# Turning and splitting the embedding's input p on VectorE during the second group of projections, and loading the parts from memory

## The chip, the cores and the metric

The kernel runs on one core of one Trainium2 chip. A core has a matrix engine (TensorE, PE in the profile; PEld is its loading of weights), VectorE (DVE), ScalarE (ACT), GpSimd (POOL) and SyncE (SP), which run beside one another and wait for each other by semaphores, and 16 DMA engines that move data between HBM and the core's memory. Matmuls write to PSUM; the other operands lie in SBUF. SP, ACT and POOL issue the DMAs, each on a queue of its own. The metric is the device time of one execution in microseconds; lower is better.

## The reference

One layer of a streaming encoder on 2048 prompt frames and 32 frames of running streams (2080 in all, 1024 wide), in fp32:

```python
hn = rmsnorm(h, g_mix)
proj = hn @ w_in                                  # (2080, 1024) @ (1024, 3072)
hA, bA, cA, zA, vB, zB = split(proj)              # a gated convolution and a pooling mixer
yA = bA * short_conv(cA * hA) * silu(zA)
yB = (pool_groups(vB) @ pool_w * pool_scale) * silu(zB)
h = h + concat(yA, yB) @ w_out                    # (2080, 1024) @ (1024, 1024)
gate = sigmoid(rmsnorm(h, g_ple) @ w_ple_gate)    # (2080, 1024) @ (1024, 1024)
h = h + (p @ w_ple) * gate                        # p: (2080, 256), w_ple: (256, 1024)
y = rmsnorm(h, g_final)
```

The change is about `p @ w_ple`, the embedding e, and about p, its input. The states of the two mixers are outputs too.

## The kernel before

Frames are handled in 17 tiles: 16 of 128 frames and one of 32. Every fp32 operand of a matmul is split in two parts of a narrower kind: `split` (L75 to L81) lets ACT copy the value to the first part (L77) and DVE subtract that from the value to give the second (L80). A product is then three matmuls, part by part. The large products go further: two by two blocks are multiplied in the manner of Strassen with seven products in place of eight (`seven`), from sums of blocks that DVE prepares.

The stages, in order of time. First, frames are normalised and turned (to 31 us). The projections follow in three groups of frame blocks, `GROUPS = [[0, 1], [2, 3], [4]]`, each with four units of output columns: group 0 to 233 us, group 1 to 427, and the plain group 2, which is block 4 alone, to 539. Then come three early tiles of the embedding (to 548), the output projection (PE line L169, to 710), the other embedding tiles but one (to 750; 12 full tiles and the short one), the gate of the short tile (`gl`, to 759) and the gate of the full tiles in pairs (to 921). The last pair (`last_pair`, L1459 ff) computes tile 15's embedding itself.

The matmuls want p with its 256 columns on the partitions. `embed` (L106 to L152) does this for a list of tiles: `prep` loads rows of p for four tiles in one DMA on SP (L123, L126), PE transposes a tile in two pieces of 128 by 128 into PSUM (L132, tile `ptp`), and `split` makes the parts `pps` from there. `run` keeps two tiles ahead, multiplies (`embed_product`, L101 to L104: two halves of 512 columns, six matmuls each), copies the result out of PSUM on ACT (L149) and writes it to e_d (L150), from where the gate stage loads it. It is called for the early tiles (`early_embedding`), for the rest (`rest_e`), and the last pair has its own copy (`embedded`, L1479).

What runs beside the units' matmuls in the projections is a generator that `at_pace` advances by a given share of steps at fixed places of a unit. In group 1, from unit j = 1 on, it is `last_block` (L1150 ff): it normalises and turns the four tiles of block 4 and writes them to b_d in memory, one step in three calls. Group 2 then loads b_d into `hn` by two DMAs on POOL's queue (L1183). The raw weights of each unit are loaded by SP and split by ACT and DVE some way ahead of PE; buffers are given out in rings (`ring4`), and a load waits until the ring's oldest buffer is free.

A scheduler orders the instructions of each engine, but an engine takes its own in order, and so do the queues: an instruction that waits holds up all behind it on its engine. Sums of squares go from ACT to POOL, which makes 1/rms from them (L69, L73); POOL also issues many of the DMAs.

For the gate, the rows of w_gate are loaded by POOL, scaled by ACT and written to g_d (`scale_gate`, L1287 to L1292), loaded again as raw weights `wg_r` by SP (L1385) and split and summed by DVE and ACT during the embedding. The frames' rows h come back from h_d: `turned` (L1388 to L1401) has PE turn them (`pth`, L1399), and `turned_here` (L1403 to L1412) loads them with 32 partitions to a piece (L1408) and has DVE turn blocks of 32 by 32 in place (`nc.vector.transpose`, L1410, STREAM_TRANSPOSE in the profile). Since blocks alone are turned, rows of the weights are taken in the order that fits, which is why w_gate is loaded by the pattern `(q k c) n -> k q c n`.

SBUF pools that the change touches: xin (5 buffers of 128x1024, rows of frames during the projections), ya (5), xh (3), cmb (8), st (4 buffers for `pps` and sums), ss (3).

Of the kernel before, what the change touches and what calls it, by code (L numbers as in the profile page):

```python
# [9 lines left out]
F32 = mybir.dt.float32  # L10
# [5 lines left out]
P = 128  # L16
D = 1024
# [17 lines left out]
def trunk(ctx, tc, x_p, x_s, c_conv, c_pool, p_p, p_s, g_mix, w_in, conv_w, conv_b, pool_w,  # L35
# [8 lines left out]
    h_d = tc.dram_tile([T, D], F32, name="h_d")  # L44
    e_d = tc.dram_tile([T, D], F32, name="e_d")
    g_d = tc.dram_tile([D, D], F32, name="g_d")

    const = ctx.enter_context(tc.tile_pool(name="const", bufs=1))
    ps_m = ctx.enter_context(tc.tile_pool(name="ps_m", bufs=6, space=PSUM))
# [5 lines left out]
    def tbank(name):  # L55
        return ps_t.tile([P, 512], F32, tag="tr", name=name)
# [46 lines left out]
            for q, (a, b) in enumerate(((0, 0), (0, 1), (1, 0))):  # L103
                nc.tensor.matmul(ps[:n], pps[:, a, k, :n], wp[k][b][:, cs], start=k + q == 0, stop=k == 1 and q == 2)  # L104

    def embed(todo, wp, ring, queue=nc.sync):  # L106

        got = {}

        def prep(c):
            if c in got or c >= len(todo):
                return
            i = todo[c]
            r, n = tiles[i]
            if c % 4 == 0:
                pt = ring("p", i)
                m = min(4, len(todo) - c)  # L120
                full = [j for j in todo[c:c + m] if j < NT - 1]
                if full:
                    nc.sync.dma_start(pt.rearrange("p (a d) -> p a d", a=4)[:, :len(full)],  # L123
                                      p_p[r:r + len(full) * P].rearrange("(a p) d -> p a d", p=P))
                if len(full) < m:
                    nc.sync.dma_start(pt[:DEC, len(full) * PLE:(len(full) + 1) * PLE], p_s)  # L126
                got["p"] = pt
            pt = got["p"][:, (c % 4) * PLE:(c % 4 + 1) * PLE]
            pps = ring("pps", i)
            ptp = tbank(f"ptp_{i}")  # L130
            for k in range(2):
                nc.tensor.transpose(ptp[:, k * P:k * P + n], pt[:n, k * P:(k + 1) * P], ident[:n, :n])  # L132
            v = ptp.rearrange("p (k t) -> p k t", k=4)[:, :2, :n]
            split(pps[:, 0, :, :n], pps[:, 1, :, :n], v)
            got[c] = pps

        def run(c, last=False):
            i = todo[c]
            r, n = tiles[i]
            prep(c)  # L140
            prep(c + 1)
            prep(c + 2)
            pps = got[c]
            o = ring("out", i)
            for nh in range(2):
                cs = slice(nh * NH, nh * NH + NH)
                ps = bank(f"e_{i}_{nh}")
                embed_product(ps, pps, wp, cs, n)
                (nc.vector.tensor_copy if last and nh else nc.scalar.copy)(o[:n, cs], ps[:n])  # L149
            (nc.gpsimd if last else queue).dma_start(e_d[r:r + n], o[:n])  # L150

        return prep, run  # L152
# [170 lines left out]
    def load_bottom(k, t):  # L323
        return nc.sync.dma_start(t, w_out[(KH + k) * P:(KH + k + 1) * P])

    def load_rows(pool, name, i, pr, sa=None):
        r, n = tiles[i]
        t = ring4(pool, f"{name}_{i}")
        nc.sync.dma_start(t[:n], pr[r:r + n] if sa is None else rows_of(pr, sa, r, n))
        return t  # L330

    with ExitStack() as s1:
# [768 lines left out]
        def embedding_weights(name):  # L1101
            wp = []
            for k in range(2):
                raw = ring4(raws, f"raw_{name}{k}")
                nc.sync.dma_start(raw, w_ple[k * P:(k + 1) * P])
                t = [wtile(f"{name}{k}_{h}").rearrange("p k h n -> p (k h n)") for h in range(2)]
                split(t[0], t[1], raw)
                wp.append(t)
            return wp
# [39 lines left out]
        def last_block():  # L1149

            load_ahead(2, 0)
            for c in range(4):
# [5 lines left out]
                for half in range(2):  # L1158
                    pt = turn(x, half, f"pt4_{c}_{half}", later=True)
                    to_memory(b_d[:, half * KH:half * KH + KH], f"b_4_{c}_{half}", pt, c * P, x[1])  # L1160
                    yield

        def at_pace(steps, num, den):

            calls = [0]

            def step():
                calls[0] += num
                while calls[0] >= den:
                    calls[0] -= den  # L1170
                    next(steps, None)

            return step

        B = B0
        for gi, tbs in enumerate(GROUPS):
            if gi == 2:

                frames_in.close()
                t = slot("hn_4")  # L1180
                hn[4] = piece_of(t, 0), piece_of(t, 1)
                for half in range(2):
                    nc.gpsimd.dma_start(hn[4][half].bitcast(F32), b_d[:, half * KH:half * KH + KH])  # L1183
                W = sums_slots("wo")
                nc.sync.dma_start(g_bc, g_fin.partition_broadcast(P))
                ya = ctx.enter_context(tc.tile_pool(name="ya", bufs=5, side="right"))
                first_y = load_y(0, 2 * P)
                first_x = load_rows(ya, "x", 0, x_p)
                tops = [ring4(ya, f"wo_q{i}") for i in range(2)]
                for k in range(KH):  # L1190
                    load_top(k, tops[k // 2])
            if gi == 1:
                B = load_group(1)
            for j in range(4):
                unit = gi * 4 + j
                u = Unit(gi, tbs, j)
                if unit == 0:
                    u.plain()
                    B0["T4"] = piece_of(seventh("B0_T4"), 0)
                    nc.sync.dma_start(B0["T4"].bitcast(F32), p_d["T4"])  # L1200
                    p_d["T4"] = tc.dram_tile([P, KH, 2, NB], F32, name="p_dT4b")
                    aside = at_pace(next_columns(3, 0, 1, 2), 39, 56)
                elif gi == 0:
                    u.seven(B, aside)
                elif gi == 1:
                    if j == 1:
                        aside = at_pace(last_block(), 1, 3)
                    u.seven(B, aside, j == 0)
                else:
                    u.plain()  # L1210
                if gi == 2:
                    early_sums(j)
# [5 lines left out]
    with ExitStack() as s2:  # L1218
# [48 lines left out]
            S[i], more = frame_parts(cmb, ss, f"y{i}", lo[:, :, :P], hi[:, :, :P], lo[:, :, P:], hi[:, :, P:])  # L1267
            return more

        def short(name, parts, n):  # L1270
            A = []
            for half, t in enumerate(parts):
                c = cmb.tile([P, KH, 2, P], F32R, tag="c", name=f"{name}_{half}")
                c = c.rearrange("p k h n -> p k (h n)")
                split(c[:, :, :n], c[:, :, n:2 * n], t[:, :, :n])
                A.append(c)
            return A
# [74 lines left out]
        def embedding_chunks(name):  # L1352
            wp = []
            for k in range(2):
                raw = ring4(ya, f"{name}r_{k}")
                nc.sync.dma_start(raw, w_ple[k * P:(k + 1) * P])
                t = [cmb.tile([P, KH, 2, P], F32R, tag="c", name=f"{name}_{k}_{h}").rearrange("p a b c -> p (a b c)")
                     for h in range(2)]
                split(t[0], t[1], raw)
                wp.append(t)  # L1360
            return wp
# [9 lines left out]
                return cmb.tile([P, D], F32, tag="c", name=f"eout_{i}")  # L1371
            return ring4(ya, f"e{what}_{i}")

        _, run = embed(rest_e, wp, ring)
        for c in range(len(rest_e) - LATE):
            run(c)

# [1 line left out]
        W = sums_slots("wg")  # L1379
        quarters("wg", W)  # L1380
        for k in range(KH):
            raw = [ring4(xh, f"wg_r{k}_{i}") for i in range(2)]
            for i in range(2):
                kk = i * KH + k
                nc.sync.dma_start(raw[i], g_d[kk * P:(kk + 1) * P])  # L1385
            whole_quarters(W, k, *raw)
            weight_sums(W, k, *raw)

        def turned(i):

            r, n = tiles[i]
            t = load_rows(ya, "hn", i, h_d).rearrange("p (q k c) -> p k q c", q=4, k=KC)
            out = []
            for half in range(2):
                pt = tbank(f"pth_{i}_{half}")
# [7 lines left out]
        def turned_here(i):  # L1403
# [1 line left out]
            r, n = tiles[i]  # L1405
            t = ring4(ya, f"hn_{i}")
            for q in range(4):
                nc.sync.dma_start(t[q * 32:q * 32 + 32].rearrange("p (g c) -> p g c", g=4),  # L1408
                                  h_d[r:r + P, q * 256:q * 256 + 256].rearrange("(g p) c -> p g c", p=32))
            nc.vector.transpose(t, t)  # L1410
            u = t.rearrange("p (g k t) -> p k g t", g=4, k=KC)
# [47 lines left out]
        def last_pair(i, A):  # L1459
# [1 line left out]

            pt = ring4(ya, "p_l")[:, :PLE]
            nc.sync.dma_start(pt, p_p[(i + 1) * P:(i + 2) * P])
            e = load_rows(ya, "e", i, e_d)
            wp = embedding_chunks("wl")
            h = [load_rows(xh, "h", i + b, h_d) for b in range(2)]
# [2 lines left out]
            hg = [ring4(ya, f"hg_{b}") for b in range(2)]  # L1471
            sums = [[], []]
            gate = {}

            def embedded():
                pps = ss.tile([P, 2, 2, P], F32R, tag="s", name="pps_l")
                ptp = tbank("ptp_l")
                for k in range(2):
                    nc.tensor.transpose(ptp[:, k * P:k * P + P], pt[:, k * P:(k + 1) * P], ident)  # L1479
                split(pps[:, 0], pps[:, 1], ptp.rearrange("p (k t) -> p k t", k=4)[:, :2])  # L1480
                return pps

            def finish(b, half, ee, m):

# [40 lines left out]
                embed_product(ps, pps, wp, slice(half * NH, half * NH + NH))  # L1525
                finish(1, half, ps, m)

            pps = embedded()
            seven(f"g{i}", A, W, carry, out, {5: lambda: second(1, NH)}, first_tile=True)
            second(0, NH // 2)  # L1530

# [36 lines left out]

        S = {}
        n = tiles[NT - 1][1]  # L1570
        A = short("gl", turned(NT - 1), n)
        for step in prep_g(0).values():
            step()
        for c in range(len(rest_e) - LATE, len(rest_e)):
            run(c)
        h, e = (load_rows(*a) for a in ((xh, "h", NT - 1, h_d), (ya, "e", NT - 1, e_d)))
# [39 lines left out]
```

## Time and profile before

| What | us |
|---|---|
| Median of 3 runs | 931.7 (931.09 to 933.5) |
| Profiled execution, device time | 930.71 |
| Its span in the profile | 928.9 |
| PE busy | 916.0 (99%), 4581 instructions |
| DVE busy | 716.7 (77%) |
| ACT busy | 483.7 (52%) |
| POOL busy | 127.5 (14%) |
| DMA packets | 133791, 190.05 MB, mean 205 GB/s |
| PE clock granted | 0.998 of full speed |

The span runs from the first to the last instruction of the profile, and the device time has 1.8 us more around it. A line of the timeline or of a group gives start, duration, engine, line of the kernel, operation and output <- inputs by the program's names; in brackets stands the idle time before it with what ended that. PE's durations overlap, because matmuls are pipelined; the distance from start to start tells what one costs. A line of the waits gives who waited for whom: us in total, times, the longest. A line of the windows gives a stretch, its length, each engine's busy time with its instructions, the clock, the mean busy share of the 16 DMA engines and GB/s.

### The profile page before, as it was taken

How to read it: one execution, taken by the hardware profiler on the slowest of the kernel's cores; microseconds unless marked ns; L12 is line 12 of the kernel's file. 1: busy time of each engine (PE TensorE's matmuls, PEld its weight loads, DVE VectorE, ACT ScalarE, POOL GpSimd, SP SyncE). 2: the span in 40 equal slices, each digit the busy share in tenths (PEclk: the TensorE clock that was granted, in tenths of full speed). 3: DMA queues.
4: the chain of work that ended last, by engine and by line, in shares of the span. 5: the costliest groups of instructions: out<-in, count | busy, mean ns of one | idle time of the engine just before them, and what ended most of it. 6: DMA issues, size and time to landing. Idle time of an engine off the chain costs nothing.

```text
span 928.9 us, 13088 instructions
## 1 busy us (share of the span) xinstructions
PE 916.0 (99%) x4581; PEld 827.6 (89%) x4581; DVE 716.7 (77%) x1215; ACT 483.7 (52%) x895; POOL 127.5 (14%) x244
## 2 busy tenths in 40 slices
PE   8999999999999999999999999999999999999996
PEld 7999999999999999999999987888878868888885
DVE  7996989999487778585777679655564797888985
ACT  7734565654345544443544356344334865555664
POOL 3011232211001110000000011112111001111113
PEclk9999999999999999999999999999999999999999
DMA  9257687798935457247665369666775883666563
GB/s 271 81 153 220 175 258 224 220 297 321 388 98 177 127 177 222 87 116 257 194 178 169 127 219 300 216 214 199 224 210 184 313 261 120 217 224 229 192 209 114
DMA packets 133791, 190.05 MB, mean 205 GB/s; under 512 B 11740, under 2 KB 101084, under 8 KB 132445
## 3 DMA queue, kind: packets, MB, share of 16 engines
q1 hardware_dynamic: 117741, 138.78, 47.7%
q0 software_dynamic: 13248, 44.93, 14.9%
q10 hardware_dynamic: 2736, 5.51, 1.9%
q8 instruction: 36, 0.59, 0.3%
q14 instruction: 30, 0.25, 0.1%
HBM read 129.59 MB, written 59.58 MB: 204 GB/s over the span
## 4 chain that ended last, share of the span: by engine, by line
PE 80%; DVE 4%; DMA 2%; ACT 1%; issue 1%; POOL 1%; SPq 0%; POOLq 0%; DVEq 0%; ACTq 0%
PE x_o L169 9%; PE x_g L169 9%; PE x_zab L580 6%; PE x_ch L580 5%; PE x_zbv L580 5%; PE e L104 5%; PE z_g L169 5%; PE z_o L169 4%; PE z_ch L580 3%; PE z_zab L580 3%; PE z_zbv L580 2%; PE y_g L169 2%; PE y_o L169 2%; PE b L580 2%; PE v L580 2%; PE c L580 2%
## 5 line engine op out<-in xcount | busy, mean ns | idle before, releaser
L77 ACT CAST y_S<-y_fS 128x512 fp32r<-128x512 f32 x32 | 19.6, 623 | 43.3 <-PE x_o L169 19.4
L104 PE MATMUL e<-wq,pps 128*128 128x512 f32 (+1 forms) x156 | 38.9, 399 | 0.2 <-ACT pps L77 0.2
L169 PE MATMUL x_g<-wg_b,g_S 128*128 128x512 f32 x128 | 36.0, 390 | 0.0
L169 PE MATMUL x_o<-wo_b,y_S 128*128 128x512 f32 x128 | 35.8, 391 | 0.0
L580 PE MATMUL x_zbv<-B,w_zbv_S 128*128 128x416 f32 x168 | 34.3, 352 | 0.0
L580 PE MATMUL z_ch<-B,w_ch_S 128*128 128x416 f32 x168 | 34.2, 352 | 0.0
L580 PE MATMUL z_zbv<-B,w_zbv_S 128*128 128x416 f32 x168 | 34.1, 351 | 0.0
L580 PE MATMUL x_zab<-B,w_zab_S 128*128 128x416 f32 x168 | 34.1, 351 | 0.0
L580 PE MATMUL z_zab<-B,w_zab_S 128*128 128x416 f32 x168 | 34.1, 351 | 0.0
L580 PE MATMUL x_ch<-B,w_ch_S 128*128 128x416 f32 x168 | 34.0, 351 | 0.0
L104 PEld LDWEIGHTS e<-wq,pps 128*128 128x128 f32 (+1 forms) x156 | 27.4, 182 | 6.9 <-ACT pps L77 0.5
L580 PEld LDWEIGHTS x_ch<-B,w_ch_S 128*128 128x128 f32 x168 | 31.4, 188 | 0.3
L580 PEld LDWEIGHTS z_zbv<-B,w_zbv_S 128*128 128x128 f32 x168 | 31.3, 188 | 0.3
L580 PEld LDWEIGHTS x_zab<-B,w_zab_S 128*128 128x128 f32 x168 | 31.3, 188 | 0.3
L580 PEld LDWEIGHTS z_zab<-B,w_zab_S 128*128 128x128 f32 x168 | 31.3, 188 | 0.3
L580 PEld LDWEIGHTS z_ch<-B,w_ch_S 128*128 128x128 f32 x168 | 31.3, 188 | 0.4
L580 PEld LDWEIGHTS x_zbv<-B,w_zbv_S 128*128 128x128 f32 x168 | 31.2, 188 | 0.4
L69 POOL TENSOR_SCALAR ms_f<-ssq_f 128x1 f32<-128x1 f32 (+1 forms) x15 | 8.8, 587 | 161.3 <-ACT junk L90 161.3
L77 ACT CAST y<-y 128x512 fp32r<-128x512 f32 x24 | 14.9, 620 | 29.2 <-PE x_o L169 14.0
L414 DVE SCALAR_TENSOR_TENSOR xt<-xt,rstd_x,g_bc 128x1024 f32<-128x1024 f32 (+2 forms) x14 | 17.9, 1280 | 15.3 <-POOL rstd_x L73 14.1
L1438 DVE SCALAR_TENSOR_TENSOR h<-h,rstd_f,g_bc 128x1024 f32<-128x1024 f32 (+1 forms) x15 | 19.3, 1284 | 12.7 <-POOL rstd_f L73 12.7
L169 PEld LDWEIGHTS x_o<-wo_b,y_S 128*128 128x128 f32 x128 | 24.0, 188 | 5.1 <-ACT c_o L1242 0.3
(583 smaller groups left out, 2664.2 us busy)
## 6 DMA issues: line engine op xcount, KB each, us to landing
y<-y_d SPq DMA_DIRECT2D x16, 512.0 KB, 10.5
x<-in_x_prompt_dram SPq DMA_DIRECT2D x16, 512.0 KB, 6.3
h_d<-x SPq DMA_DIRECT2D x16, 512.0 KB, 4.2
h<-h_d SPq DMA_DIRECT2D x16, 512.0 KB, 3.6
xt<-in_x_prompt_dram SPq DMA_DIRECT2D x15, 512.0 KB, 7.3
e<-e_d SPq DMA_DIRECT2D x15, 512.0 KB, 5.8
out_dram<-h POOLq DMA_DIRECT2D x14, 512.0 KB, 3.0
p_dT<-T POOLq DMA_DIRECT2D x12, 512.0 KB, 6.1
```

Source lines behind the costliest of these rows:

```text
L69: nc.gpsimd.tensor_scalar(ms[:n], ssq[:n], scalar1=1.0 / D, scalar2=EPS, op0=ALU.mult, op1=ALU.add)
L77: ins = nc.scalar.copy(hi, src)
L104: nc.tensor.matmul(ps[:n], pps[:, a, k, :n], wp[k][b][:, cs], start=k + q == 0, stop=k == 1 and q == 2)
L169: nc.tensor.matmul(ps[:n], lhs[:, k, a, :n], w[b][:, k], start=start and k + q == 0, stop=k == KH - 1 and q == 2, skip_group_check=True)
L414: nc.vector.scalar_tensor_tensor(xt[:n], xt[:n], r[:n], g_bc[:n], op0=ALU.mult, op1=ALU.mult)
L580: nc.tensor.matmul(ps[:, :NB], lhs[:, k, x], b[:, k, y], start=start and k + q == 0, stop=stop and k == KH - 1 and q == 2, skip_group_chec ...
L1438: nc.vector.scalar_tensor_tensor(h[:n], h[:n], rf[:n], g_bc[:n], op0=ALU.mult, op1=ALU.mult)
```

## The change

p is turned and split once, during group 1, and the parts are kept in memory (pp_d). A generator `turn_p` follows `last_block` in group 1, and the two together advance one step in two calls. It works in five rounds, four of four tiles and one of the short tile. POOL's queue loads p's rows in four pieces of 32 partitions, DVE turns blocks of 32 by 32 in place (128x1024, or 128x64 for the short tile), ACT and DVE split tile by tile, and POOL's queue writes each tile's parts, 256 KB, to pp_d. The next round's load is issued behind the turn of the one before.

In the embedding, `prep` only loads a tile's parts from pp_d: on SP for the three early tiles, on POOL's queue for the others, on SP for the last pair's. `run` looks four tiles ahead in place of three. The transposes L132 and L1479, their PSUM tiles and the splits behind them are gone. The rows of w_ple are loaded in the order that the turned blocks have (`ple_rows`).

To make room and order for this, the raw weights of the gate take buffers of ya and xh in turn in place of xh alone, the short gate's parts lie in ya in place of cmb, and the first loads of hn for the gate (short tile and first pair) go to POOL's queue, later ones to SP as before. Since turn_p keeps xin in use until its end, the pool ya, which takes the same room, and with it the first loads of y, x and wo_q for the output projection, begin later in SP's order: behind raw_v of group 2, where they stood between the raw weights of unit 3 before.

```diff
+    pp_d = tc.dram_tile([NT, P, 2 * PLE], F32, name="pp_d")
...
+    ple_rows = w_ple.rearrange("(q k c) n -> k q c n", q=4, k=2)
+
+    def load_pps(t, i, queue):
+        n = tiles[i][1]
+        queue.dma_start(t.rearrange("p a k n -> p (a k) n")[:, :, :n].bitcast(F32),
+                        pp_d[i].rearrange("p (a n) -> p a n", a=4)[:, :, :n])
+        return t
...
-    def embed(todo, wp, ring, queue=nc.sync):
+    def embed(todo, wp, ring, queue=nc.sync, loads=nc.sync):
...
-            ptp = tbank(f"ptp_{i}")
-            for k in range(2):
-                nc.tensor.transpose(ptp[:, k * P:k * P + n], pt[:n, k * P:(k + 1) * P], ident[:n, :n])
-            v = ptp.rearrange("p (k t) -> p k t", k=4)[:, :2, :n]
-            split(pps[:, 0, :, :n], pps[:, 1, :, :n], v)
-            got[c] = pps
+            if c not in got and c < len(todo):
+                got[c] = load_pps(ring("pps", todo[c]), todo[c], loads)
...
-            prep(c)
-            prep(c + 1)
-            prep(c + 2)
+            for ahead in range(4):
+                prep(c + ahead)
...
-                nc.sync.dma_start(raw, w_ple[k * P:(k + 1) * P])
+                nc.sync.dma_start(raw, ple_rows[k])
...
+        def turn_p():
+
+            def load(a):
+                t = ring4(xin, f"p_{a}")
+                for q in range(4):
+                    part, cs = t[q * 32:q * 32 + 32], slice(q * 64, q * 64 + 64)
+                    if a < NT - 1:
+                        nc.gpsimd.dma_start(part.rearrange("p (m c) -> p m c", c=64),
+                                            p_p[a * P:(a + 4) * P, cs].rearrange("(m p) c -> p m c", p=32))
+                    else:
+                        nc.gpsimd.dma_start(part[:, :64], p_s[:, cs])
+                return t
+
+            rounds = [*range(0, NT - 1, 4), NT - 1]
+            t = load(0)
+            yield
+            for a, after in zip(rounds, rounds[1:] + [None]):
+                w = D if a < NT - 1 else 64
+                nc.vector.transpose(t[:, :w], t[:, :w])
+                v = t[:, :w]
+                if after is not None:
+                    t = load(after)
+                yield
+                for b in range(0, 4 if w == D else 1, 2):
...
+                        split(hi, lo, src)
+                        nc.gpsimd.dma_start(pp_d[i].rearrange("p (a n) -> p a n", a=4)[:, :, :n],
+                                            o.rearrange("p a k n -> p (a k) n").bitcast(F32))
                     yield
...
-                        aside = at_pace(last_block(), 1, 3)
+                        aside = at_pace(chain(last_block(), turn_p()), 1, 2)
...
-        _, run = embed(rest_e, wp, ring)
+        _, run = embed(rest_e, wp, ring, loads=nc.gpsimd)
...
-            raw = [ring4(xh, f"wg_r{k}_{i}") for i in range(2)]
+            raw = [ring4(t, f"wg_r{k}_{i}") for i, t in enumerate(((ya, ya), (ya, xh), (xh, xh), (ya, ya))[k])]
...
+        hn_queue = [nc.gpsimd]
...
-            pt = ring4(ya, "p_l")[:, :PLE]
-            nc.sync.dma_start(pt, p_p[(i + 1) * P:(i + 2) * P])
+            pps = load_pps(ss.tile([P, 2, 2, P], F32R, tag="s", name="pps_l"), i + 1, nc.sync)
...
-            pps = embedded()
             seven(f"g{i}", A, W, carry, out, {5: lambda: second(1, NH)}, first_tile=True)
...
-        A = short("gl", turned(NT - 1), n)
+        A = short("gl", turned(NT - 1), n, ya)
         for step in prep_g(0).values():
             step()
+        hn_queue[0] = nc.sync
```

More of the change, by code (lines that the diff above doesn't have):

```diff
@@ L104, in embed_product @@
                 nc.tensor.matmul(ps[:n], pps[:, a, k, :n], wp[k][b][:, cs], start=k + q == 0, stop=k == 1 and q == 2)
-    def embed(todo, wp, ring, queue=nc.sync):
+    ple_rows = w_ple.rearrange("(q k c) n -> k q c n", q=4, k=2)
[5 more added lines that the diff above has]
+    def embed(todo, wp, ring, queue=nc.sync, loads=nc.sync):
         got = {}
         def prep(c):
[L114 to L129, printed above, removed]
-            ptp = tbank(f"ptp_{i}")
-            for k in range(2):
-                nc.tensor.transpose(ptp[:, k * P:k * P + n], pt[:n, k * P:(k + 1) * P], ident[:n, :n])
-            v = ptp.rearrange("p (k t) -> p k t", k=4)[:, :2, :n]
-            split(pps[:, 0, :, :n], pps[:, 1, :, :n], v)
-            got[c] = pps
+            if c not in got and c < len(todo):
+                got[c] = load_pps(ring("pps", todo[c]), todo[c], loads)
         def run(c, last=False):
@@ L324, in load_bottom, with load_rows @@
         return nc.sync.dma_start(t, w_out[(KH + k) * P:(KH + k + 1) * P])
-    def load_rows(pool, name, i, pr, sa=None):
+    def load_rows(pool, name, i, pr, sa=None, queue=nc.sync):
         r, n = tiles[i]
         t = ring4(pool, f"{name}_{i}")
-        nc.sync.dma_start(t[:n], pr[r:r + n] if sa is None else rows_of(pr, sa, r, n))
+        queue.dma_start(t[:n], pr[r:r + n] if sa is None else rows_of(pr, sa, r, n))
         return t
@@ L1161, in last_block @@
                     yield
+        def turn_p():
[20 more added lines that the diff above has]
+                for b in range(0, 4 if w == D else 1, 2):
+                    s = staged(f"pps_{a + b}").rearrange("p a h n -> p (a h n)")
+                    for c in range(2 if w == D else 1):
+                        i = a + b + c
+                        n = tiles[i][1]
+                        o = s[:, c * 2 * PLE:(c + 1) * 2 * PLE].rearrange("p (a k n) -> p a k n", a=2, k=2)[:, :, :, :n]
+                        if n == P:
+                            src = v[:, (b + c) * PLE:(b + c + 1) * PLE].rearrange("p (g k r) -> p k g r", g=4, k=2)
+                            hi, lo = (o[:, h].rearrange("p k (g r) -> p k g r", g=4) for h in range(2))
+                        else:
+                            src = v.rearrange("p (k r) -> p k r", k=2)
+                            hi, lo = o[:, 0], o[:, 1]
+                        split(hi, lo, src)
+                        nc.gpsimd.dma_start(pp_d[i].rearrange("p (a n) -> p a n", a=4)[:, :, :n],
+                                            o.rearrange("p a k n -> p (a k) n").bitcast(F32))
+                    yield
         def at_pace(steps, num, den):
@@ L1268, in prep_h, with short @@
             return more
-        def short(name, parts, n):
+        def short(name, parts, n, pool=None):
             A = []
+            if pool is not None:
+                both = pool.tile([P, 2, KH, P], F32R, tag="t", name=f"{name}_a")
             for half, t in enumerate(parts):
-                c = cmb.tile([P, KH, 2, P], F32R, tag="c", name=f"{name}_{half}")
-                c = c.rearrange("p k h n -> p k (h n)")
+                c = (cmb.tile([P, KH, 2, P], F32R, tag="c", name=f"{name}_{half}").rearrange("p k h n -> p k (h n)")
+                     if pool is None else both[:, half])
                 split(c[:, :, :n], c[:, :, n:2 * n], t[:, :, :n])
@@ L1355, in embedding_chunks @@
                 raw = ring4(ya, f"{name}r_{k}")
-                nc.sync.dma_start(raw, w_ple[k * P:(k + 1) * P])
+                nc.sync.dma_start(raw, ple_rows[k])
                 t = [cmb.tile([P, KH, 2, P], F32R, tag="c", name=f"{name}_{k}_{h}").rearrange("p a b c -> p (a b c)")
@@ L1387, in trunk @@
             weight_sums(W, k, *raw)
+        hn_queue = [nc.gpsimd]
         def turned(i):
             r, n = tiles[i]
-            t = load_rows(ya, "hn", i, h_d).rearrange("p (q k c) -> p k q c", q=4, k=KC)
+            t = load_rows(ya, "hn", i, h_d, queue=hn_queue[0]).rearrange("p (q k c) -> p k q c", q=4, k=KC)
             out = []
@@ L1407, in turned_here @@
             for q in range(4):
-                nc.sync.dma_start(t[q * 32:q * 32 + 32].rearrange("p (g c) -> p g c", g=4),
+                hn_queue[0].dma_start(t[q * 32:q * 32 + 32].rearrange("p (g c) -> p g c", g=4),
                                   h_d[r:r + P, q * 256:q * 256 + 256].rearrange("(g p) c -> p g c", p=32))
@@ L1473, in last_pair @@
             gate = {}
[L1475 to L1481, printed above, removed]
             def finish(b, half, ee, m):
```

## The prediction

> **What bounds the kernel now.** I read the page first, then TensorE's waits, then the timeline of the stretch that the change shortens. The page has TensorE (PE) busy for 916.0 of 928.9 us:
>
> ```profile
> span 928.9 us, 13088 instructions
> ...
> PE 916.0 (99%) x4581; PEld 827.6 (89%) x4581; DVE 716.7 (77%) x1215; ACT 483.7 (52%) x895; POOL 127.5 (14%) x244
> ```
>
> The chain of waits gives PE 80%. PE's own waits, by what ended them, are short and nearly all early:
>
> ```profile
> PE gm L376 <- DVE V L813: 2.3, 1, 2.3
> PE zb L608 <- DVE B L654: 0.8, 1, 0.8
> PE y_o L164 <- ACT wo_c L1308: 0.5, 1, 0.5
> ...
> PE e L104 <- ACT pps L77: 0.2, 1, 0.2
> ```
>
> So the time is the sum of what PE issues. Work taken off PE counts in full, and work put on other engines costs nothing until PE waits for it. The timeline of PE from 704 us shows what the transposes of p cost there (start, length, line, what, count; lengths overlap, so I go by the distance of starts):
>
> ```profile
> 704.74 2.88 PE L169 MATMUL z_o<-wo_d,y_S 128*128 128x512 f32 x12
> 707.46 2.89 PE L169 MATMUL x_o<-wo_T,y 128*128 128x512 f32 x12
> ...
> 710.19 0.60 PE L132 MATMUL ptp<-ident,ep 128*128 128x128 f32 x4
> 711.03 0.96 PE L104 MATMUL e<-wq,pps 128*128 128x512 f32 x3 [0.24 <-ACT pps L77]
> ...
> 717.14 0.38 PE L132 MATMUL ptp<-ident,ep 128*128 128x128 f32 x2
> 717.27 3.00 PE L104 MATMUL e<-wq,pps 128*128 128x512 f32 x12
> 720.11 0.38 PE L132 MATMUL ptp<-ident,ep 128*128 128x128 f32 x2
> ```
>
> Twelve matmuls of 512 columns take 707.46 − 704.74 = 2.72 us in the output projection. A tile of the embedding has the same twelve and a pair of transposes, and takes 720.11 − 717.14 = 2.97 us. A pair costs **0.25 us**: 0.14 of its own and 0.11 by which the matmuls behind it start later.
>
> **What is removed from PE.** The order of the changed program's instructions has none of the 17 pairs: 13 in the embedding's main stretch, 3 in its early tiles, one in the last pair of gate tiles. 17 × 0.25 = 4.25 us. The main stretch also loses its first wait: the last of the four transposes at 710.19 starts at 710.51 and its follower at 711.03, 0.52 us against the 0.07 between others, so 0.45 more. Sum **4.7 us**. From above: the stretch is 40.24 us (710.19 to 750.43); less 156 matmuls at 0.2267 = 35.37, and less 0.61 for the eight transposes of hn at 744.19, it leaves 4.26 for 13 pairs and the wait, which with 4 × 0.25 for the others is 5.3. From below: if the matmuls behind a pair start late for a reason that stays, 17 × 0.14 + 0.45 = 2.8. I take 4.7, since 2.97 against 2.72 repeats at every tile. The 17 ACT copies (375 ns) and 17 DVE subtracts (422 ns) also leave these stretches; neither bounds them, ACT being busy 32.07 of 40 us there and DVE 29.02.
>
> **What is added, in the second group (277 to 427 us).** DVE: four stream transposes of 128x1024, by the same instruction on hn (1237 ns), one short, and 17 subtracts of 128x256. 4 × 1.24 + 0.2 + 17 × 0.42 = 12.3 us; ACT 17 × 0.375 = 6.4. Room, by windows (PE, PEld, DVE, ACT, POOL busy):
>
> ```profile
> 290.00:325.00 35.00, 35.00 (x192) 34.49 (x191) 26.77 (x41) 19.09 (x34) 5.21 (x8) 1.00 0.54 160
> 325.00:360.00 35.00, 35.00 (x191) 33.69 (x190) 26.54 (x44) 15.92 (x30) 4.86 (x6) 1.00 0.55 157
> 360.00:393.00 33.00, 33.00 (x176) 32.67 (x176) 22.50 (x40) 14.03 (x26) 0.00 (x0) 1.00 0.55 176
> 393.00:427.00 34.00, 34.00 (x182) 33.66 (x181) 25.80 (x38) 15.00 (x26) 1.12 (x2) 1.00 0.52 179
> ```
>
> DVE idles 35.4 us from 290 to 427, and PE never does. What is queued behind a round of the new work is the weights' splits. They end 9 to 13 us before PE's first matmul on them (w_zbv_S: split done 331.00, first used 339.99; most others 11.6 to 13.1), and that lead is nearly constant, so it is set by buffers that PE gives back, not by DVE. A round is 1.24 + 4 × 0.42 = 2.9 us, inside it. I take nothing; the end on the other side is all 12.3 us on PE. POOL's loads and writes of p (some 0.5 to 1 us to issue each, as b_d's writes) add p's 2.1 MB and 4.2 MB of writes to a stretch where DMA is 0.54 busy. The norms of the moved block 4 queue on POOL behind them; PE's transposes of it stand far ahead of their use at 427, and a late one could cost some tenths.
>
> **What is moved.** (1) The loads of y, x and wo_q for the next stage (2.5 MB, SP, 356 to 367 us now) take the room that p's rows held, so they start behind the last write of p's parts, near 405. They are used after 548: no cost by themselves. They fall, however, next to the load of block 4:
>
> ```profile
> 416.36 1.15 POOL L1183 DMA_DIRECT2D hn<-b_d  x2 [62.08 <-PE y_zab L580]
> ```
>
> Its data end at 428 and PE needs the halves at 427.2 and 429.5, so it has about 1.2 us of cover. DMA moved 406 GB/s there at most, so 2.5 MB in front is 6.2 us, 5.0 beyond the cover. I take nothing, as SP reaches them about 10 us before 416. (2) Three early loads of the parts on SP wait for parts 0 to 2 to land, near 357 by the pace worked out below; behind them stands raw_ch_3a, split at 382, now loaded at 361: 15 us of cover. (3) The main stretch loads each tile's parts (256 KB, POOL) when a buffer of four comes free, three tiles before use: 3 × 2.72 = 8.2 us. POOL's loads have these rows: the median of gs (256 KB) is 8.5 us from issue to landing, 5.6 to 12.2; hn<-b_d (1.66 MB) 7.0 and 11.8; its writes of 512 KB about 3. At 701 to 702 us gs runs alone, with 30% of the 16 engines busy and 94 GB/s, while hn<-b_d keeps 96% busy at 406 GB/s. The parts have 128 plain rows like hn, so 0.65 us of data in place of gs's 2.8: 8.5 − 2.1 = 6.4 us, an estimate, within 8.2. No cost; by gs's longest, 12.2, each of nine tiles would wait (12.2 + 2.72 − 4 × 2.72) / 4 = 1.0 us, 9 in all. (4) w_ple is read in permuted row groups, as w_gate is for gs. For 512 KB that is 5.6 us at 94 GB/s against 1.3 at 406, 4.3 more per load. The first two sets have 11 and 23 us of lead. The last pair's second half is issued at 900.66, split by 909.4 and used at 916.2, 6.8 later: with 4.3 more it still comes 2.5 us early. (5) The loads of the gate's raw weights, earlier now, help DVE, not PE. A wait of 0.29 us at 764.66, behind ACT's table load, may go; I count nothing.
>
> The rule behind (4) is in the Trainium skill, "DMA: Bandwidth & Descriptors", section "Why a DMA increments its semaphore by 16 and not by 1": a DMA is spread over the largest number of engines up to 16 that divides the slowest dimension of both its sides. By it these loads, whose slowest dimension is 4, use 4 engines. The 30% of gs agrees (4 of 16 are 25%, and one engine's packet lies across the edge of the window).
>
> **Sum.** 928.9 − 4.7 = 924.2 span; the profiled execution took 930.71, so 926.0. The median is 931.7, 1.0 above the profiled one; by it **927.0**. With 5.3 and the 0.29 gone it is 926.1, and 925 if the 1.1 us that PE loses at 559 (y_o, behind ACT's copies of wo_c) goes too; with 2.8 it is 928.9.
>
> **Rivals.** *Given back (no change).* The load of block 4 is pushed by the moved loads: 5.0 us, 932.0. Or transfers bind the main stretch: it moves 11.8 MB in 40 us now, and nine to thirteen loads of parts make 14.1 to 15.2; at 406 GB/s the larger is 37.4 us against PE's 36.5, and hn's loads for the gate, which queue behind the parts on POOL, come later by what is saved or more: 3.7 returned, 930.7. For it: DMA is 0.84 busy there already. Against: most of the gate's raw weights may now move ahead of 710, where queues stand empty at 705 to 708. *Wl is late:* the loads in gs's row order take longer than its 94 GB/s make them. Each us past the 2.5 of cover delays e_l; at two thirds of that rate it is 2.8 us more and e_l 0.3 late, at half 5.6 more and 3.1 late, 930.1 *Slower.* DVE takes its work in order, and a stream transpose waits for p's rows, which come through POOL's queue in 256-byte pieces. Once such a wait and its round exceed the splits' lead of 9 to 13 us, PE waits for weights. It decides from a load that lands more than 9 − 2.9 = 6 us after DVE reaches the transpose; at worst the 12.3 us come on top: 931.7 + 12.3 − 4.7 = 939. For it: gs shows loads of 12 us on that queue, and p's rows are smaller. Against: each load is issued a round ahead. The writes of b_d stand 20 us apart for the three steps of a block at one step in three calls (290.8, 310.4, 330.6), so at one in two a round of three steps takes some 13 us. *The change does not do what it says:* the order of instructions excludes it.
>
> **How the numbers follow.** A difference under 0.3% (2.8 us) is not told from none. Forecast 0.62 (925 to 928.9); given back 0.18 (929 to 932.3); wl late 0.06, most of it still faster; slower 0.14. Faster 0.66, same 0.20, slower 0.14. The range runs from 925.0 to 932.3, which leaves out the slower case and little else.
>
> **What would show it.** Right: no ptp on PE, 2.72 us between tiles of e, the stretch 36 to 36.6 us, the second group's PE without waits, pps loads landing within 8 us. Wrong: PE waits on DVE's weight splits between 325 and 427, on hn near 427, on pps in the main stretch, or on hn and g_S at its end; e_l waiting for wl.

## The result, and the profile after

The changed kernel takes 942.99 us (939.15 to 944.53, 6 runs) against 933.34 us (931.09 to 934.33, 6 runs) for the kernel before on the same chip: a ratio of 1.0101, with a 95% interval of 1.0087 to 1.0116. It is slower by 9.7 us, outside the predicted range and on the other side. Its profiled execution took 943.32 us, with a span of 941.5. From the page:

```profile
span 941.5 us, 13162 instructions
...
PE 918.1 (98%) x4547; PEld 828.9 (88%) x4547; DVE 718.6 (76%) x1220; ACT 483.9 (51%) x895; POOL 160.1 (17%) x300
```

PE has 34 instructions less, the transposes, and yet it is busy for longer and idle for 23.4 us in place of 12.9. Its waits in the changed kernel (who waited for whom, us in total, times, longest):

```profile
PE z_o L158 <- DVE c_o L1266: 5.0, 1, 5.0
PE pm L822 <- ACT pp L78: 2.4, 1, 2.4
PE gm L365 <- DVE V L802: 2.3, 1, 2.3
PE x_g L158 <- ACT c_g L1452: 1.4, 2, 1.0
```

Three of the four are new, and none of them is a wait for p's parts, for weight splits or for hn. The distances between the same matmuls in both traces say what each stage takes (us). The two spans differ by 12.6 us, more than the medians do, since the profiled execution of before was a quick one (930.71 us, against its median of 933.34): the start alone, which the change leaves as it was, took between 14.3 and 16.1 us over all the traces.

| From, to | before | after | four pieces (e1) |
|---|---|---|---|
| start to the first zb | 14.3 | 16.0 | 16.0 |
| first zb to block 4's zb | 413.0 | 414.0 | 414.1 |
| block 4's zb to the first early e | 112.1 | 117.5 | 111.5 |
| early e to the first x_o | 8.5 | 8.4 | 8.4 |
| first x_o to the last of the output projection | 162.1 | 168.9 | 162.0 |
| from there to the short gate | 40.5 | 36.8 | 36.9 |
| short gate to e_l | 165.1 | 166.4 | 165.1 |
| e_l to the end | 13.4 | 13.5 | 13.3 |

The embedding's stretch gives what was forecast, 3.7 us. On PE's timeline its tiles now stand without a gap, 44 matmuls in 10.14 us, which is 2.7 for twelve:

```profile
722.32 2.88 PE L158 MATMUL x_o<-wo_T,y 128*128 128x512 f32 x12
725.04 10.14 PE L105 MATMUL e<-wq,pps 128*128 128x512 f32 x44
```

The loss is in stretches where the prediction saw no cost: 5.3 us between block 4's zb and the early embedding, 6.8 in the output projection, 1.4 in the gate (the last two rows together). The chain of waits says who came late there. In the first of them (start, length, what):

```profile
522.03 7.62 DMA wo_r<-in_w_out_dram
529.64 0.02 issue
529.67 0.69 DVE wo_r L168
```

DVE takes its work in order and stands at the difference of two blocks of w_out (L168) until their load lands. Behind it are the pooling's sums, which PE needs as pp at 531.9. In the output projection:

```profile
675.46 15.18 DMA x<-in_x_prompt_dram
690.64 0.03 issue
...
690.73 0.70 DVE c_o L1266
```

A load of 512 KB takes 15.2 us, where the same load of x took 6.5 before (666.96 to 673.41). Both late loads stand directly behind, or between, two loads of w_ple on SP: raw_wp at 512.92 and 517.45 ahead of wo_r at 522.03, wqr at 673.38 and 676.47 around x at 675.46. The DMA engines meanwhile have little to do. For 682 to 686 us the DMA view has (the lines of a queue give packets, MB and share of 16 engines):

```profile
DMA packets 112, 0.40 MB, mean 101 GB/s; under 512 B 4, under 2 KB 4, under 8 KB 112
...
q1 hardware_dynamic: 47, 0.19, 11.9%
q0 software_dynamic: 42, 0.17, 11.1%
q10 hardware_dynamic: 23, 0.04, 2.6%
```

A quarter of the engines is busy, and 101 GB/s is moved, where 406 was seen elsewhere. SP's queue (q1) and POOL's (q0, the gs loads) share that quarter evenly. So this looks like loads that lie on four engines and hold up the four shares of a load that is spread over all sixteen.

In the gate it is the last pair: ACT waits 2.95 us for the second half of wl, and the copies of x_g out of PSUM, which PE needs, are queued on ACT behind that cast.

### The profile page after: what moved, and what is told of

Same layout as the page of the kernel before. It is cut to its first block, busy times and chain, and to the rows that moved or that the text cites. A ratio compares the mean times of both kernels' runs of the same rounds, so it can differ in the third digit from the quotient of the medians.

```text
span 941.5 us, 13162 instructions
## 1 busy us (share of the span) xinstructions
PE 918.1 (98%) x4547; PEld 828.9 (88%) x4547; DVE 718.6 (76%) x1220; ACT 483.9 (51%) x895; POOL 160.1 (17%) x300
## 4 chain that ended last, share of the span: by engine, by line
PE 57%; DMA 4%; DVE 3%; ACT 1%; issue 1%; POOL 0%; POOLq 0%; ACTq 0%; DVEq 0%
PE x_g L158 8%; PE x_o L158 7%; PE e L105 5%; PE z_g L158 4%; PE z_o L158 4%; PE x_zab L569 3%; PE x_ch L569 2%; PE za L569 2%; PE y_g L158 2%; PE x_zbv L569 2%; PE b L569 2%; PE zb L569 2%; DMA x<-in_x_prompt_dram 2%; PE v L569 2%; PE z_zab L569 1%; PE y_o L158 1%
## 5 line engine op out<-in xcount | busy, mean ns | idle before, releaser
L158 PE MATMUL x_g<-wg_b,g_S 128*128 128x512 f32 x128 | 36.9, 393 | 1.0 <-ACT c_g L1452 1.0
L105 PE MATMUL e<-wq,pps 128*128 128x512 f32 (+1 forms) x156 | 36.2, 391 | 0.0
L158 PEld LDWEIGHTS x_g<-wg_b,g_S 128*128 128x128 f32 x128 | 23.7, 188 | 6.1 <-ACT c_g L1452 1.4
```

The source lines that it names most:

```text
L158: nc.tensor.matmul(ps[:n], lhs[:, k, a, :n], w[b][:, k], start=start and k + q == 0, stop=k == KH - 1 and q == 2, skip_group_check=True)
```

## The experiments

Theory A: the six loads of w_ple, in row groups of four, run on about 4 of 16 DMA engines, and other loads wait for these 4. Rival B: the moved loads of y, x and wo_q, the new rooms, or the traffic of the parts make wo_r and x late.

**e1, four pieces.**

```diff
-                nc.sync.dma_start(raw, ple_rows[k])
+                for q in range(4):
+                    nc.sync.dma_start(raw[q * 32:q * 32 + 32], w_ple[q * 64 + k * 32:q * 64 + k * 32 + 32])
```

> The changed kernel, but each load of 128 rows of w_ple is made as four loads of 32 rows that lie together (24 short loads in place of 6; the same rows in the same places). Theory A (the six loads in row groups run on about 4 of the 16 DMA engines, and what SP's queue has behind them, wo_r before 531 us, x before 690 us, waits for those 4): the waits of PE at 531 and 686 us and ACT's at 920 go, that is 5.3 + 0.6 for the stretch from zb to the early embedding, 6.8 for the output projection and 1.4 + 0.25 for the gate, 14 in all, 943.0 to 929 us (927 to 932), below before. Rival B (the moved loads of y, x and wo_q, the new rooms, or the traffic of the parts make wo_r and x late): 943, 941 to 945, with the waits at 531 and 686 still there.

Measured: 929.18 us (928.76 to 930.92) against 932.92; ratio 0.9961, interval 0.9949 to 0.9974. 13.8 us less than the changed kernel, and faster than the one before. The stretches are in the table above. PE's waits there:

```profile
PE pt L410 <- DVE xt L617: 2.1, 1, 2.1
...
PE z_g L158 <- ACT c_g L1454: 0.4, 1, 0.4
...
PE e L105 <- DMA pps<-pp_d: 0.2, 1, 0.2
```

The waits for c_o and pp are gone; the 2.1 for xt lies before the first zb. All that the change moved or added, other than the row pattern of six loads, is still in this kernel, so rival B falls.

**e2, the slowest dimension 32.**

```diff
-    ple_rows = w_ple.rearrange("(q k c) n -> k q c n", q=4, k=2)
+    ple_rows = w_ple.rearrange("(q k c) n -> k c q n", q=4, k=2)
```

> The changed kernel with one word of the row pattern turned: (q k c) n -> k c q n in place of k q c n. The same 128 rows per load, in one DMA, but the slowest of the pattern's dimensions is 32 and not 4, and the rows come to other partitions, so that the embedding multiplies rows that do not belong together. Theory A: as for the four pieces, 929 us (927 to 932), and the loads move over 300 GB/s. Rival B: 943. A rival C, that the scattered rows as such are slow and not the number of engines: 943 as well, with w_ple loads near 100 GB/s, while the four pieces recover.

Measured: 929.19 us (928.5 to 930.58), ratio 0.9961 (0.9945 to 0.9976). It has the same six DMAs and the same rows as the changed kernel, and no row lies beside its neighbour; only the order of the pattern's dimensions differs. Around the first of its six loads 393 GB/s pass, a write of y_d among them (514.5 to 516 us, shown below). So neither scattered rows nor the number of DMAs is the cause, and rival C falls.

**e8 and e9, slowest dimensions 2 and 8.**

```diff
-    ple_rows = w_ple.rearrange("(q k c) n -> k q c n", q=4, k=2)
+    ple_rows = w_ple.rearrange("(k e c) n -> k c e n", k=2, c=2)     # e8; c=8 in e9
```

> The changed kernel with another row order in the w_ple loads: 128 rows of each half of w_ple, whose slowest dimension is 2 in place of 4; rows come to other partitions, so that the embedding multiplies rows that do not belong together. If the slowest dimension sets the number of DMA engines, two carry each load, 47 GB/s and 11 us per load in place of 94 and 5.6; x lands some 11 us later than the 690.7 of the changed kernel, wo_r and wl 5 to 10 later: 943 + 15 to 27 = 958 to 970. If it is only the scattered rows, 943.

> The same with a slowest dimension of 8. If it sets the number of engines, eight carry each load, 188 GB/s and 2.8 us; the pair ahead of x costs 5.6 us less, and the waits at 531 and 686 shrink to 0 to 1 us each: 929 to 933. If it is only the scattered rows (each row alone here, 4 KB as before), 943.

Measured: with 2, 968.33 us (967.93 to 971.02), ratio 1.0393 (1.0377 to 1.0410); with 8, 932.24 us (929.03 to 934.66), ratio 0.9996 (0.9982 to 1.0010). With 4 it was 943 and with 32, 929. How many engines such a load keeps busy can be read off where SP's queue has only the two early loads of w_ple under way, in the windows of e8 (2), the changed kernel (4) and e9 (8); the last line is e2 (32), with the write of y_d. The last three numbers are the clock, the share of the 16 DMA engines and GB/s:

```profile
516.00:519.00 3.00, 3.00 (x18) 2.97 (x17) 1.02 (x2) 1.02 (x2) 0.00 (x0) 1.00 0.13 53
516.00:519.00 3.00, 3.00 (x18) 2.97 (x17) 0.69 (x1) 1.27 (x3) 0.00 (x0) 1.00 0.26 85
520.00:521.50 1.50, 1.50 (x10) 1.49 (x9) 0.69 (x1) 0.62 (x1) 0.00 (x0) 1.00 0.49 134
514.50:516.00 1.50, 1.50 (x9) 1.48 (x9) 0.24 (x1) 0.62 (x1) 0.00 (x0) 1.00 0.99 393
```

13, 26 and 49% of 16 are two, four and eight engines. What each of them moves is not the same: 26 GB/s with two, 21 with four (25 at 682 us above), 17 with eight, so that eight give 134 GB/s and not the 188 expected. The waits of PE in e8 are the same three, larger:

```profile
PE pm L822 <- ACT pp L78: 11.6, 1, 11.6
PE x_g L158 <- ACT c_g L1452: 8.9, 2, 5.5
PE z_o L158 <- DVE c_o L1266: 8.4, 1, 8.4
```

In e9 PE still waits 2.2 us for c_o, more than expected (x takes 12.7 us there), and no longer for pp.

**e3, the row pattern alone in the kernel before.**

```diff
-                nc.sync.dma_start(raw, w_ple[k * P:(k + 1) * P])
+                nc.sync.dma_start(raw, ple_rows[k])
```

> The kernel before, with its six loads of w_ple in the row order of the change (k q c n) and nothing else; the embedding then multiplies rows that do not belong together. Theory A: slower than before by the wait for x near 690 (4 to 7 us), up to 1.7 in the last pair and 0 to 4 near 531, where DVE's order has the sum of wo_r behind the pooling: 938 to 946. Rival B: as before, 933 (within 1.5).

Measured: 944.38 us (942.93 to 945.6), ratio 1.0120 (1.0106 to 1.0134). The six loads alone make the kernel before 11.5 us slower, more than the whole change did, which has its gain against them. Here the output projection is 7.1 us longer and the gate 5.1 (x lands after 15.5 us in its chain of waits), and the stretch before the early embedding not at all: in that order of DVE the work on wo_r stands behind the pooling.

**e4, four pieces for the main stretch's two loads only.** The edit of e1, under `if name == "wq"`.

> The changed kernel with the four pieces for the main stretch's two loads of w_ple alone (wq); those of the early tiles and the last pair stay in row groups of 4. Theory A: only the wait at 686 goes, 943.0 - 6.8 = 936 us (934.5 to 938), and PE still waits for pp near 531 and ACT for wl near 920. Rival B: 943.

Measured: 937.42 us (935.2 to 938.79), ratio 1.0044 (1.0030 to 1.0058). The output projection is back at 162.0 us, and PE still waits 2.4 us for pp and 0.9 for c_g: each site has its own price.

**e6, on POOL's queue.** `nc.gpsimd.dma_start(raw, ple_rows[k])` in the changed kernel.

> The changed kernel with its six w_ple loads still in row groups of 4, but issued on POOL's queue and not on SP's. Theory A1 (a load waits behind the w_ple loads because both stand in SP's rings, and the rings of another queue are served in turn): the waits at 531 and 686 go, 929 to 933 us, x lands within 8 us, though the w_ple loads themselves stay slow, near 100 GB/s. Theory A2 (the 4 engines as such are taken, whatever queue the load stands on): x and wo_r stay late, 940 to 944.

Measured: 940.82 us (938.48 to 942.98), ratio 1.0093 (1.0074 to 1.0113). x still takes 13.1 us and PE still waits 3.0 for c_o and 2.0 for pp. A1's forecast failed: another queue does not cure it. That the four engines alone are the reason in this run is not shown: nearly all of the 16 DMA engines' time is taken there from 681 to 688 us (64.4% by SP's queue, 33.9 by POOL's), at 231 GB/s. So whether x waits in SP's own order or for the engines as such stays open. PE also waits 1.9 us for block 4's hn in e6, which no other run shows and which is not explained.

**e5 and e7, the pace of p's steps**, on top of e1, after a wait of 0.7 us that both the changed kernel and e1 have near 304 us.

```diff
-                        aside = at_pace(chain(last_block(), turn_p()), 1, 2)
+                        aside = at_pace(chain(twice(last_block()), turn_p()), 2, 3)     # e5
+                        aside = at_pace(chain(thrice(last_block()), turn_p()), 1, 1)    # e7
```

`twice` and `thrice` spread each step of `last_block` over two or three.

> The four pieces, and block 4's turning keeps its old pace of one step in three calls, p's steps follow at two in three. The theory: the 0.8 us that PE loses near 304 us (pt waits for DVE's xt, DVE for POOL's rstd_x) comes from the faster pace, at which a normalisation and the turn of its tile stand two calls apart and not three; it goes, 929.2 to 928.4. The rival: p's own work in group 1 makes it late; then it stays, 929.2, and since p's steps now follow closer to each other, PE waits for weight splits or for pp appear between 340 and 427.

> The four pieces; block 4's turning at its old pace of one step in three calls, then p's steps at one per call, so that p's last write comes near 395 us (401 in the four pieces, 420 in the run with p at two in three). The theory from that run: what cost 7.5 us there was the late end of p's work, since the loads of y, x and wo_q, and after them raw_c and raw_za, stand behind it on SP and beside hn<-b_d; with the early end no wait near 430 to 455 appears, and the 0.8 us at 304 is gone: 928.4 us (927 to 930). The rival, DVE: with a round of p's work in half the time the weight splits come late and PE waits for them between 340 and 400, 930 to 936.

Measured: e5 936.4 us (934.18 to 937.05), ratio 1.0041 (1.0026 to 1.0055); e7 937.64 us (935.51 to 938.31), ratio 1.0053 (1.0040 to 1.0067). The wait at 304 goes in both, as the theory had it, and shows in no total: between the first zb and block 4's the two take 414.2 and 414.9 us against e1's 414.1, with a longer wait in group 0 (pt_g, 1.3 us in place of 0.5), which the edit does not touch. Both lose 7.5 to 8.4 us to e1 between block 4's zb and the early embedding, where PE does not wait in e1. The last write of p's parts is issued at 420 in both, against 401 in e1, in e7 too, where I had expected 395: p's rounds stayed 12.5 to 17 us apart whatever the pace, for a reason that I did not find. What follows the late end is seen on SP's queue in e5:

```profile
420.58 0.38 SPq L506 DMA_DIRECT2D raw_c<-in_w_in_dram  x1
...
423.94 10.24 SPq L305 DMA_DIRECT2D y<-y_d  x2
...
440.86 0.43 SPq L506 DMA_DIRECT2D raw_za<-in_w_in_dram  x1
```

SP stands 10 us at the loads of y, which take the room that p held; raw_za is issued at 440.86 in place of 420.42 in e1, raw_c takes 14.6 us beside hn<-b_d, and PE waits 3.9 us for pp near 450. In e7 PE waits 4.5 us for pp, but SP stands elsewhere, 7.4 us at raw_za and 3.3 at raw_b, and the load of wo_r, on which DVE waits, follows at 441.33 in place of 437.44; what holds SP there is not shown. The weight splits in group 1 are not late in either.

## Why the prediction was wrong

**The term of PE was right.** Forecast −4.7. e1 shows −3.5 in the main stretch and −0.7 around the early tiles. The 0.25 of the last pair is taken back there by a wait of 0.4 for c_g. Together −4.2, and 3.7 by the medians (932.92 to 929.18). The span of e1 is only 1.5 less than that of before, because the profiled execution of before was a quick one: in e3 and e1 alike the start is 1.8 us later, and e3, which does none of p's work, also loses 0.8 up to block 4's zb.

**The step that failed is (4), "w_ple is read in permuted row groups".** Its rate was about right (94 GB/s; the early loads of the changed kernel moved 85, and 101 passed at 682), with some luck, since two loads of gs, issued at 697.14 and 698.44, were under way in the microsecond that it was read from. The page's rule that stood beside it, in "DMA: Bandwidth & Descriptors" of the Trainium skill, is borne out by 2, 4, 8 and 32, with 13, 26, 49 and 99% of the engines busy. What was wrong is whom I charged. I compared each slow load with the use of its own data, 11 and 23 us away, and found cover. I did not ask what stands behind it on SP and on those engines: wo_r and x, with covers of a few us. I had looked at the loads behind moved instructions everywhere else in the sum. In the last pair I did see the load, and two things were wrong. It was priced at 5.6 us as if alone, and took 10.3 from issue to landing, the first half being under way until 913. And I counted only up to e_l's use of it: ACT, waiting 2.95 us for it, held back two copies out of PSUM that PE needed sooner. The rival "wl is late" had the right load and the right reason (it takes longer than 94 GB/s make it), but only e_l as the one who waits, and a chance of 0.06.

**One wait cost nearly double.** PE waits 2.4 us for pp, and behind that the clock falls. In the windows (PE busy, PEld, DVE, ACT, POOL, then the granted clock):

```profile
532.00:536.00 4.00, 1.40 (x3) 0.96 (x4) 3.86 (x12) 1.61 (x3) 0.00 (x0) 0.75 0.38 131
536.50:542.00 5.50, 5.50 (x20) 5.27 (x20) 4.92 (x13) 2.54 (x5) 0.00 (x0) 0.61 0.11 39
```

za's 24 matmuls stand 346 ns apart at first, against 189 in e1, and take 6.7 us in place of 4.5: 2 us more, without a wait. The 5.0 us that PE waits for c_o are followed in the same way: of z_o's next matmuls the first seven take 3.0 us, where seven take 1.6 at full clock. That makes 6.4 of the 6.8.

**The rest.** Of the slower rival, DVE's work in order, nothing was seen: in e1 the stream transposes find p's rows landed (no idle time before any of them) and no split of weights is late. The loads of the parts in the main stretch landed in time (0.2 us of waiting in e1, against "no cost"). Block 4's hn was not late in the changed kernel or in e1, though the cover that the prediction gave its second half was too large: it landed at 428.8 in the kernel before, for a use at 429.5, so 0.7 us and not 1.2. e5 and e7 show that the step was the right one to fear: with p's end 19 us later it costs 7.5 to 8.4 us, though not by hn but by loads that SP issues later or that take longer, in e5 behind its stand at y. The 0.7 us near 304, PE's transposes of block 4 waiting for a norm behind POOL, is the "some tenths" of the moved block 4.

## What to carry to other kernels

Look at the slowest dimension of every DMA pattern that a change touches (the runs here varied it on the side of HBM): a rearranged row order can put a load on two or four of sixteen engines, and turning the order of the dimensions, or cutting the load in pieces of whole rows, brings it back. When a transfer gets slower, ask first what is issued behind it, and only then when its own data are used. And when a change with a sound gain comes out slower, compare the stages by the distance of the same matmuls: here the gain stood in full where it was meant to be, and e1 keeps it.

## What the runs showed of the hardware

- A load from HBM whose pattern there has 2, 4 or 8 as its slowest dimension kept 13, 26 and 49% of the 16 DMA engines busy and moved 53, 85 and 134 GB/s; with 32 it was 99% and 393 GB/s. On POOL's queue two such loads with 4 took 9.9 and 10.4 us from issue to landing (raw_wp in e6), against 4.2 for one with 32 on SP's (e2). A load over all engines issued between two loads with 4 took 15.2 us in place of 6.5.
- A wait of 2.4 us, in 4 us in which PE was busy for 1.4, lowered the granted clock to 0.61 over the next 5.5 us. The Trainium skill ("TensorE: Matmul & The Clock Gate", part 1) has half clock after an idle window of about 3.4 us; slots of 346 for 189 ns agree with about half, and here a shorter wait was enough.
